# GpSimd rounds the weights' high parts beside the two top-256 searches of a hybrid attention block

## The chip, the cores and the metric

One core of a Trainium2 chip runs the kernel. Its engines are TensorE (PE; weight loads stand apart as PEld), VectorE (DVE), ScalarE (ACT), GpSimd (POOL) and SyncE (SP, which only issues DMAs). The metric is the device time of one execution in microseconds. The program is laid out by a scheduler: the Python code says what is to be done, and the scheduler sets the order in which each engine's instructions stand; on the chip each engine then works its queue in that order, and waits at its head.

## The reference, cut to what matters

The block takes x (1024 rows of 1024) through a mixer with two branches and through an MLP:

```python
h = rms_norm(x, g_mix[l]) * (1 + sc1) + sh1
proj = jnp.einsum('bsd,de->bse', h, w_in[l])
p_a, p_b = proj[..., :N_IN_A], proj[..., N_IN_A:]
...
# branch A, for each block of 128 queries: the 256 best keys by an index score
score_idx = jnp.where(key_pos[None, :] < limit[:, None], score_idx, -jnp.inf)
_, sel = lax.top_k(score_idx, topk)
...
# branch B: RWKV-7 time mixing on p_b, chunk by chunk
x = x + gt1 * jnp.einsum('bse,ed->bsd', mixed, w_out[l])
h = rms_norm(x, g_ffn[l]) * (1 + sc2) + sh2
u = jax.nn.relu(jnp.einsum('bsd,df->bsf', h, w_ff1[l]))
x = x + gt2 * jnp.einsum('bsf,fd->bsd', u * u, w_ff2[l])
```

## The kernel before, in words

The sequence is worked in two halves of 512 rows (`hf` 0 and 1). All matrices with a weight go through `dense` (line 406). It takes the weight in loads of 512 rows by 128 columns, and each load is split: `load_w` (line 393) fetches it with one DMA on SP into `wraw` (5 buffers), rounds it to a high part `whi`, and subtracts to get a low part `wlo` (4 buffers each). The activations are split in the same way (hh and hl, or uh and ul), and `dense` runs three matmuls of 128x128 by 512 columns for each 128 rows: hi with hi, hi with lo, lo with hi. So one load feeds 12 matmuls, and a group of two loads, 24 matmuls, fills one PSUM tile `ps_mm`, of which there are two. Before the change ACT makes every `whi` in one cast of 128x512 (line 399), and `wlo` is made on POOL in two subtractions of 128x256 (helper `InHalves`, line 136), in the second half's MLP on DVE (line 401). The table `LE` says which, by a number `GRP[0]` that the caller sets: 0 and 2 in `rwkv_proj` for the two halves (line 475), 1 and 3 in `attn_proj`, 4 and 5 in `out_proj`, 6 and 7 in `ffn`.

The top-256 choice is made in `indexer` (line 846) by a search over the 32 bits of the threshold: in each bit a candidate threshold is set, the scores at or above it are counted, and the bit is kept or dropped. Half of the query blocks are counted by DVE: `jk` (line 937 for the upper 16 bits on bf16 copies, line 939 for the lower 16 on the f32 scores and a zero tile), then `acc`, `pre` and `cand` on two columns (lines 952, 953, 928). The others are counted by ACT: `jka` (line 931), and then DVE makes `acca`, `prea` and `canda` (lines 946, 954, 929), and ACT's next count waits for `canda`. The first search, of `hf` 0, has one block on each engine. The second, of `hf` 1, has two on each (640 and 768 columns on DVE, 896 and 1024 on ACT). When the bits are done DVE builds the masks (lines 957 to 986), and `attention` starts.

The first search runs beside `rwkv_proj(1, hT1)`, that is 14 groups, 28 loads, of `w_in`; there ACT scales the group's result (`sh`, line 439) and DVE adds the shifted row (`shy`, line 443), which frees the PSUM tile. The second runs beside the first quarters of `ffn(0, ...)`. Its hidden columns go in four quarters `fg`; each has eight groups `f` of `w_ff1` (line 1114), whose result ACT takes out as relu (`ur`, line 1118), squares (line 1132) and rounds (`uh`, line 1133), and DVE subtracts (`ul`, line 1134), and then eight groups `d` of `w_ff2` (line 1139), whose result DVE adds to `xT` (line 1140). A quarter is 32 loads. A group `d` needs all eight uh and ul of its quarter.

Of the kernel before, what the change touches and what calls it, by code (L numbers as in the profile page):

```python
# [32 lines left out]
LS = 1  # L33
VB = (0, 1)
VB0 = 0
LE = 'gggggggv'
HE = 'aaaaaaaa'
DL = -1
PO = (1, 0, 2)
# [72 lines left out]
def body(tc, I, out, dbg=None):  # L112
    nc = tc.nc
    V, G, A, T = nc.vector, nc.gpsimd, nc.scalar, nc.tensor
# [26 lines left out]
    def mark(n):  # L141
        MK[0] = n
# [250 lines left out]
    def load_w(w, row0, col0, M):  # L393

        raw = wp.tile([128, 4, 128], F32, name="wraw", tag="wraw", bufs=WB[0])
        nc.sync.dma_start(raw[:, :, 0:M], w[row0:row0 + 512, col0:col0 + M].rearrange("(k p) n -> p k n", p=128))
        hi = wp.tile([128, 4, 128], F32R, name="whi", tag="whi", bufs=WB[1])
        lo = wp.tile([128, 4, 128], F32R, name="wlo", tag="wlo", bufs=WB[1])
        (A.copy if HE[GRP[0]] == "a" else V.tensor_copy)(hi[:, :, 0:M], raw[:, :, 0:M])  # L399
        GRP[1] ^= 1  # L400
        (V if LE[GRP[0]] == "v" or LE[GRP[0]] == "m" and GRP[1] else InHalves).tensor_tensor(lo[:, :, 0:M], raw[:, :, 0:M], hi[:, :, 0:M].bitcast(F32), ALU.subtract)  # L401
        return hi, lo

    GRP = [0, 0]
# [684 lines left out]
    def ffn(hf, xT, hT, fp, xp, hid, hooks={}):  # L1089
# [14 lines left out]
        def hook(unit):  # L1104
            for h in hooks.get(unit, ()):
                h()
                mark('ffn%d' % hf)
            GRP[0] = 6 + hf

        for fg in range(FF // 128 // GF):  # L1110
            uh, ul = [], []
            for f in range(GF):
                hook(16 * fg + f)
                ps = dense(I["w_ff1"], 0, 8, (fg * GF + f) * 128, 128,
                           lambda k: hT[0][:, k, :], lambda k: hT[1][:, k, :])
                r = fp.tile([128, HALF], F32, name="ur", tag="s2", bufs=sb(fp))
                if RL[hf] == "a":
                    A.activation(r, ps, AF.Relu)
                else:
                    V.tensor_scalar(r, ps, 0.0, None, ALU.max)  # L1120
                if f < 4:
                    ta, tb = (("shy", "fsq"), ("shy", "fsq"), ("sh1", "arn"), ("sh1", "cT"))[f]
                    a = dp.tile([128, HALF], F32R, name="uh", tag=ta, bufs=2)
                    b = dp.tile([128, HALF], F32R, name="ul", tag=tb, bufs=2 if f < 2 else 1)
                else:
                    a = hid.tile([128, HALF], F32R, name="uh", tag="uh", bufs=4)
                    b = hid.tile([128, HALF], F32R, name="ul", tag="ul", bufs=4)
                if SQ[hf] == "v":
                    A.activation(a, r, AF.Square)
                    V.tensor_tensor(r, r, r, ALU.mult)  # L1130
                else:
                    A.activation(r, r, AF.Square)
                    A.copy(a, r)  # L1133
                V.tensor_tensor(b, r, a.bitcast(F32), ALU.subtract)  # L1134
                uh.append(a)
                ul.append(b)
            for d in range(8):
                hook(16 * fg + 8 + d)
                ps = dense(I["w_ff2"], fg * GF * 128, GF, d * 128, 128, lambda k: uh[k], lambda k: ul[k])
                V.scalar_tensor_tensor(xT[:, d, :], ps, mod[:, 40 + d:41 + d], xT[:, d, :], ALU.mult, ALU.add)  # L1140
                if hf and fg == FF // 128 // GF - 1 and d in (5, 7):
                    store(d // 6)
# [217 lines left out]
```

## Time and profile before

| | |
|---|---|
| median of 3 runs | 1782.42 us (1778.94 to 1782.9) |
| the profiled execution: its own time | 1785.96 us |
| the profiled execution: its span, first to last instruction | 1784.2 us |
| granted TensorE clock, mean of the span | 0.972 |
| busy: PE, DVE, ACT, POOL | 1616.8, 1047.8, 878.1, 565.8 us |
| `whi` casts on ACT (line 399) | 384, 235.6 us |
| `wlo` subtractions on POOL (line 136) | 512, 404.4 us |
| first search: DVE's counts | about 414 to 469 us of the span |
| second search: DVE's counts, ACT's counts | about 890 to 995, to 1054 us |

Times below are microseconds from the start of the profiled execution's span. Busy time of PE is modelled and overlaps from one matmul to the next, so the number of matmuls in a stretch tells more than their busy time; a few records are missing. A wait is put down to the instruction that released it last. [...]

### The profile page before, as it was taken

The numbers are of one execution on the slowest core, as the hardware profiler recorded it, in microseconds if no ns is written. First come the engines' busy times: TensorE is split into PE (matmuls) and PEld (weight loads), VectorE is DVE, ScalarE is ACT, GpSimd is POOL, SyncE is SP. The second block draws the span as 40 slices with busy tenths as digits, with TensorE's granted clock in tenths as the row PEclk, the third lists the DMA queues.
The fourth block names the chain that finished last, engine by engine and source line by source line (L and its number), as shares of the span: only waits on it lengthen the run. The fifth ranks groups of instructions, "written<-read, shape, count | busy, mean of one in ns | idle before, by whom it ended". The sixth has DMA issues, their size and how long they took to land. (4 is left out here: it accounts for less than half of the span.)

```text
span 1784.2 us, 27312 instructions
## 1 busy us (share of the span) xinstructions
PE 1616.8 (91%) x9380; PEld 1217.4 (68%) x9380; DVE 1047.8 (59%) x2701; ACT 878.1 (49%) x1840; POOL 565.8 (32%) x751
## 2 busy tenths in 40 slices
PE   5997888988879988899968899999999999999998
PEld 2776655666655566666646676777886788888887
DVE  3786578559877676646999558763114233333333
ACT  3334364555637654535755865765235252525251
POOL 2555334353451344153224454113554300000000
PEclk9998999999999999999979999999999999999999
DMA  8895234333443441322112234324332333333332
GB/s 298 275 302 152 79 103 137 123 106 105 136 114 100 151 146 60 107 65 71 54 42 83 65 101 118 95 72 151 104 96 70 115 116 95 100 95 94 95 98 79
DMA packets 264018, 203.90 MB, mean 114 GB/s; under 512 B 17300, under 2 KB 218004, under 8 KB 263879
## 3 DMA queue, kind: packets, MB, share of 16 engines
q1 hardware_dynamic: 253122, 182.90, 34.1%
q10 hardware_dynamic: 10628, 19.24, 2.9%
q8 instruction: 74, 1.21, 0.3%
q14 instruction: 66, 0.53, 0.1%
q0 software_dynamic: 128, 0.01, 0.0%
HBM read 173.32 MB, written 28.78 MB: 113 GB/s over the span
## 5 line engine op out<-in xcount | busy, mean ns | idle before, releaser
L136 POOL TENSOR_TENSOR wlo<-wraw,whi 128x256 fp32r<-128x256 f32 x512 | 404.4, 813 | 590.7 <-ACT whi L399 493.2
L121 PE MATMUL ps_mm<-hh,whi 128*128 128x512 f32 (+1 forms) x1024 | 420.1, 411 | 27.2 <-ACT whi L399 7.1
L399 ACT CAST whi<-wraw 128x512 fp32r<-128x512 f32 x384 | 235.6, 616 | 423.9 <-PE ps_mm L121 385.9
L121 PE MATMUL ps_mm<-hl,whi 128*128 128x512 f32 (+1 forms) x1024 | 419.1, 409 | 4.2 <-DVE hl L345 1.9
L121 PE MATMUL ps_mm<-hh,wlo 128*128 128x512 f32 (+1 forms) x1024 | 414.2, 405 | 0.1
L121 PEld LDWEIGHTS ps_mm<-hh,whi 128*128 128x128 f32 (+1 forms) x1024 | 195.7, 192 | 75.0 <-ACT whi L399 16.7
L121 PEld LDWEIGHTS ps_mm<-hl,whi 128*128 128x128 f32 (+1 forms) x1024 | 196.7, 192 | 48.9 <-issue 6.8
L121 PEld LDWEIGHTS ps_mm<-hh,wlo 128*128 128x128 f32 (+1 forms) x1024 | 196.2, 192 | 42.8 <-issue 4.7
L121 PE MATMUL ps_mm<-uh,whi 128*128 128x512 f32 x512 | 204.9, 400 | 16.4 <-ACT whi L399 6.3
L121 PE MATMUL ps_mm<-ul,whi 128*128 128x512 f32 x512 | 204.4, 399 | 6.1 <-DVE ul L1134 6.1
L121 PE MATMUL ps_mm<-uh,wlo 128*128 128x512 f32 x512 | 203.9, 398 | 0.2
L401 DVE TENSOR_TENSOR wlo<-wraw,whi 128x512 fp32r<-128x512 f32 x128 | 88.2, 689 | 130.0 <-ACT whi L399 128.9
L931 ACT ACTIVATE jka<-sc,canda 128x1024 bf16<-128x1024 f32 (+1 forms) x93 | 90.2, 970 | 77.4 <-DVE canda L929 52.2
L121 PEld LDWEIGHTS ps_mm<-uh,whi 128*128 128x128 f32 x512 | 97.5, 191 | 43.1 <-issue 11.4
L121 PEld LDWEIGHTS ps_mm<-ul,whi 128*128 128x128 f32 x512 | 97.8, 191 | 28.9 <-DVE ul L1134 7.3
L121 PEld LDWEIGHTS ps_mm<-uh,wlo 128*128 128x128 f32 x512 | 97.6, 191 | 23.9 <-POOL wlo L136 1.7
L1140 DVE SCALAR_TENSOR_TENSOR xT<-ps_mm,mod,xT 128x512 f32<-128x512 f32 x64 | 47.8, 748 | 109.7 <-PE ps_mm L121 109.7
L1134 DVE TENSOR_TENSOR ul<-ur,uh 128x512 fp32r<-128x512 f32 x64 | 44.6, 697 | 80.1 <-ACT uh L1133 80.1
L1039 DVE CUSTOM_DVE_ANT_0 L<-ps_f,mk 128x512 f32<-128x512 f32 (+3 forms) x96 | 51.6, 551 | 26.6 <-PE ps_f L121 13.2
L1045 ACT ACTIVATE L<-L,m 128x128 f32<-128x128 f32 (+7 forms) x64 | 49.6, 776 | 19.5 <-DVE m L1042 14.4
L720 ACT COPY Ub<-ps_c 64x64 f32<-64x64 f32 x128 | 26.3, 205 | 65.5 <-DVE UV L718 56.9
L291 DVE SCALAR_TENSOR_TENSOR macc<-mraw,cs,macc 128x512 f32<-128x512 f32 x56 | 49.9, 890 | 10.0 <-DMA mraw<-in_w_ada_dram 8.5
(329 smaller groups left out, 2602.0 us busy)
## 6 DMA issues: line engine op xcount, KB each, us to landing
wraw<-in_w_ff_dram SPq DMA_DIRECT2D x256, 256.0 KB
wraw<-in_w_in_dram SPq DMA_DIRECT2D x92, 256.0 KB
mraw<-in_w_ada_dram SPq DMA_DIRECT2D x64, 256.0 KB
mraw<-in_w_ada_dram SPq DMA_DIRECT2D x16, 512.0 KB
wraw<-in_w_out_dram SPq DMA_DIRECT2D x32, 256.0 KB
rkvd<-shy ACTq DMA_DIRECT2D x24, 256.0 KB
xin<-in_x_dram SPq DMA_DIRECT2D x8, 512.0 KB
rt<-rnd SPq DMA_DIRECT2D x32, 128.0 KB
```

The source lines that it names most:

```text
L121: r = T.matmul(out, lhsT, rhs, start=start, stop=stop, **kw)
L136: G.tensor_tensor(o[:, c], a[:, c], b[:, c], op)
L291: V.scalar_tensor_tensor(acc, raw, c, acc, ALU.mult, ALU.add)
L399: (A.copy if HE[GRP[0]] == "a" else V.tensor_copy)(hi[:, :, 0:M], raw[:, :, 0:M])
L401: (V if LE[GRP[0]] == "v" or LE[GRP[0]] == "m" and GRP[1] else InHalves).tensor_tensor(lo[:, :, 0:M], raw[:, :, 0:M], hi[:, :, 0:M].bitcas ...
L720: (V.tensor_copy if CE[2] == "v" else A.copy)(Ub[h * 64:h * 64 + 64, h, :], pu[u, h * 64:h * 64 + 64])
L931: A.activation(jka[:, 0:width(b)], sc[b], AF.Sign, scale=-1.0, bias=0.0 if bit == 31 else canda.bitcast(F32)[:, i:i + 1], accum_out=ca[:, ...
L1039: V.tensor_tensor_reduce(L[:, c0:c0 + n], ps[:, 0:n], masks[b][:, c0:c0 + n], 1.0, -3e38, ALU.add, ALU.max, m2[:, pc:pc + 1])
L1045: A.activation(L[:, 0:W], L[:, 0:W], AF.Exp, bias=m2[:, 2:3], accum_out=m2[:, 3:4])
L1134: V.tensor_tensor(b, r, a.bitcast(F32), ALU.subtract)
L1140: V.scalar_tensor_tensor(xT[:, d, :], ps, mod[:, 40 + d:41 + d], xT[:, d, :], ALU.mult, ALU.add)
```

## The change

Where the first search runs (`GRP[0]` 2, all of `rwkv_proj(1, ...)`) and in the first two of the four quarters of `ffn(0, ...)` (a new group number 8), `whi` is no longer cast by ACT in one instruction of 512 columns but by POOL in two of 256. These are 28 and 64 loads. `wlo` stays on POOL in two subtractions. Nothing else in the code changes; the scheduler lays the program out anew.

```diff
-LE = 'gggggggv'
+LE = 'gggggggvg'
...
-        (A.copy if HE[GRP[0]] == "a" else V.tensor_copy)(hi[:, :, 0:M], raw[:, :, 0:M])
+        if GRP[0] in (2, 8):
+            for k in (0, 2):
+                G.tensor_copy(hi[:, k:k + 2, 0:M], raw[:, k:k + 2, 0:M])
+        else:
+            A.copy(hi[:, :, 0:M], raw[:, :, 0:M])
...
                 hook(16 * fg + f)
+                GRP[0] = 8 if not hf and fg < 2 else 6 + hf
                 ps = dense(I["w_ff1"], 0, 8, (fg * GF + f) * 128, 128,
...
                 hook(16 * fg + 8 + d)
+                GRP[0] = 8 if not hf and fg < 2 else 6 + hf
                 ps = dense(I["w_ff2"], fg * GF * 128, GF, d * 128, 128, lambda k: uh[k], lambda k: ul[k])
```

How the instructions stand in a row is shown at three places. The changed file is a few lines longer, so a line of it has a higher number (937 is 941, 939 is 943, 946 is 950, 952 is 956, 1118 is 1123, 1134 is 1139, 1140 is 1146).

POOL from the end of the second half's RWKV branch to the end of the second search, before (`ob` is the branch's output, `r` belongs to the norm ahead of the MLP, `klo` is a DMA that `attention(1)` needs):

```order
187 L136 TENSOR_TENSOR ob<-ob,bvs 128x256 x2
188 L136 TENSOR_TENSOR wlo<-wraw,whi 128x256 x12
189 L184 TENSOR_TENSOR r_8696<-r_8696,mhalf 128x4
190 L136 TENSOR_TENSOR wlo<-wraw,whi 128x256 x122
191 L995 DMA klo_9620<-in_spos_dram 1x16x64
192 L995 DMA klo_9621<-in_spos_dram 1x16x64
193 L136 TENSOR_TENSOR wlo<-wraw,whi 128x256 x128
```

POOL in the changed program, at the second search's end; above these rows the pairs of CAST and TENSOR_TENSOR alternate in the same way from row 241 on:

```order
361 L136 TENSOR_TENSOR wlo<-wraw,whi 128x256 x2
362 L401 CAST whi<-wraw 128x256 x2
363 L136 TENSOR_TENSOR wlo<-wraw,whi 128x256 x2
364 L401 CAST whi<-wraw 128x256
365 L999 DMA klo_9648<-in_spos_dram 1x16x64
366 L999 DMA klo_9649<-in_spos_dram 1x16x64
367 L401 CAST whi<-wraw 128x256
368 L136 TENSOR_TENSOR wlo<-wraw,whi 128x256 x2
```

Each load is now four instructions on POOL, two casts and two subtractions, one load after the other, and the DMA of `klo` stands between two casts, 63 instead of 67 loads behind the last `ob`.

ACT where DVE's counts of the second search end, before (`sc_8766` and `sc_8767` are the scores of ACT's two blocks; `ur` from `ps_mm` is the relu that frees a PSUM tile):

```order
956 L931 ACTIVATE jka,ca<-sc_8766,canda 128x896
957 L399 CAST whi<-wraw 128x512
958 L931 ACTIVATE jka,ca<-sc_8767,canda 128x1024
959 L399 CAST whi<-wraw 128x512
960 L931 ACTIVATE jka,ca<-sc_8766,canda 128x896
961 L1118 ACTIVATE ur<-ps_mm 128x512
962 L931 ACTIVATE jka,ca<-sc_8767,canda 128x1024
963 L1132 ACTIVATE ur<-ur 128x512
964 L399 CAST whi<-wraw 128x512
965 L931 ACTIVATE jka,ca<-sc_8766,canda 128x896
966 L1133 CAST uh<-ur 128x512
```

ACT at the same place in the changed program:

```order
897 L935 ACTIVATE jka,ca<-sc_8794,canda 128x896
898 L935 ACTIVATE jka,ca<-sc_8795,canda 128x1024
899 L935 ACTIVATE jka,ca<-sc_8794,canda 128x896
900 L1123 ACTIVATE ur<-ps_mm 128x512
901 L935 ACTIVATE jka,ca<-sc_8795,canda 128x1024
902 L1137 ACTIVATE ur<-ur 128x512
903 L935 ACTIVATE jka,ca<-sc_8794,canda 128x896
904 L1138 CAST uh<-ur 128x512
905 L935 ACTIVATE jka,ca<-sc_8795,canda 128x1024
906 L1123 ACTIVATE ur<-ps_mm 128x512
```

The casts of `whi` are gone from between the counts. A group of the MLP now stands beside three counts; in the rows before it stands beside two or three, with two casts more.

DVE where the first quarter passes from `w_ff1` to `w_ff2`, before (`ul` is that of the quarter's last group `f`, `xT` that of its first group `d`; `top_9198` and `top_9200` are the bf16 copies of DVE's two blocks):

```order
1576 L952 TENSOR_SCALAR acc<-cv 128x2
1577 L954 TENSOR_TENSOR prea<-prea,acca 128x2
1578 L953 TENSOR_TENSOR pre<-pre,acc 128x2
1579 L929 SCALAR_TENSOR_TENSOR canda<-prea,xma 128x2
1580 L1134 TENSOR_TENSOR ul<-ur,uh 128x512
1581 L928 SCALAR_TENSOR_TENSOR cand<-pre,xmh 128x2
1582 L937 TENSOR_SCALAR jk,cv<-top_9198,cand 128x640
1583 L937 TENSOR_SCALAR jk,cv<-top_9200,cand 128x768
1584 L1140 SCALAR_TENSOR_TENSOR xT<-ps_mm,mod,xT 128x512
```

DVE at the same place in the changed program:

```order
1579 L941 TENSOR_SCALAR jk,cv<-top_9226,cand 128x640
1580 L1139 TENSOR_TENSOR ul<-ur,uh 128x512
1581 L941 TENSOR_SCALAR jk,cv<-top_9228,cand 128x768
1582 L950 TENSOR_SCALAR acca<-ca 128x1
1583 L956 TENSOR_SCALAR acc<-cv 128x2
1584 L957 TENSOR_TENSOR pre<-pre,acc 128x2
1585 L932 SCALAR_TENSOR_TENSOR cand<-pre,xmh 128x2
1586 L941 TENSOR_SCALAR jk,cv<-top_9226,cand 128x640
1587 L1146 SCALAR_TENSOR_TENSOR xT<-ps_mm,mod,xT 128x512
```

Counted by the `acc` rows, `ul` has moved ahead by one bit of the search, and `xT` stands in the same bit; the seven `xT` that follow stand two bits apart in both programs. Where DVE's own counts end, 21 instead of 23 and 50 instead of 52 `canda` rows stand above in the program before and the changed one, in that order, for the first search and the second.

## Rows read from the trace of the kernel before

**Rows 1.** Windows view: busy us (instructions) by engine, PEclk, DMA share, GB/s.

```profile
405.00:475.00 70.00, 59.97 (x234) 45.44 (x232) 64.69 (x283) 40.50 (x89) 26.94 (x35) 0.93 0.39 113
...
885.00:940.00 55.00, 39.87 (x140) 30.03 (x139) 53.05 (x160) 28.75 (x54) 17.86 (x22) 0.81 0.16 48
940.00:988.00 48.00, 41.86 (x171) 32.58 (x170) 46.81 (x129) 27.32 (x50) 21.02 (x25) 0.96 0.24 72
988.00:1041.00 53.00, 46.26 (x189) 35.60 (x188) 20.92 (x79) 49.02 (x92) 22.45 (x31) 0.97 0.25 73
...
1055.00:1091.00 36.00, 28.91 (x123) 22.33 (x122) 35.52 (x55) 8.20 (x13) 21.30 (x23) 1.00 0.44 125
...
1250.00:1784.00 534.00, 525.08 (x2312) 423.69 (x2310) 175.85 (x257) 197.43 (x328) 81.81 (x111) 1.00 0.33 96
```

**Rows 2.** Waits of PE, 880 to 1000, then 1000 to 1060: total, times, longest.

```profile
PE ps_mm L121 <- ACT whi L399: 9.7, 3, 3.9
PE ps_mm L121 <- DVE ul L1134: 4.4, 1, 4.4
...
PE ps_mm L121 <- ACT whi L399: 3.7, 2, 2.1
```

**Rows 3.** Timeline of PE after the first of these waits: start, us, instruction [idle before].

```profile
905.52 0.80 PE L121 MATMUL ps_mm<-hh,whi 128*128 128x512 f32 x1 [3.34 <-ACT whi L399]
...
906.54 0.63 PE L121 MATMUL ps_mm<-hh,wlo 128*128 128x512 f32 x1
...
906.97 0.63 PE L121 MATMUL ps_mm<-hh,whi 128*128 128x512 f32 x1
```

**Rows 4.** Timeline of ACT ahead of it.

```profile
901.66 1.04 ACT L931 ACTIVATE jka<-sc,canda 128x896 bf16<-128x896 f32 x1 [3.61 <-DVE canda L929]
...
904.86 0.61 ACT L399 CAST whi<-wraw 128x512 fp32r<-128x512 f32 x1
```

**Rows 5.** Line 1134 on DVE, 885 to 935: ns min/median/max, first and last start.

```profile
L1134 DVE TENSOR_TENSOR ul<-ur,uh x4: 684/686/1130, 899.0 to 930.5; 128x512 fp32r<-128x512 f32 x4
```

**Rows 6.** Timeline of DVE: `acc` beside POOL's work, then `acc` and a count without.

```profile
946.23 0.58 DVE L952 TENSOR_SCALAR acc<-cv 128x2 int32<-128x2 f32 x1
...
951.17 0.15 DVE L952 TENSOR_SCALAR acc<-cv 128x2 int32<-128x2 f32 x1
...
951.75 0.88 DVE L939 SCALAR_TENSOR_TENSOR jk<-sc,cand,zer 128x640 bf16<-128x640 f32 x1
```

**Rows 7.** Groups of DVE, 885 to 988: xcount | busy us, mean ns | idle before.

```profile
L939 DVE SCALAR_TENSOR_TENSOR jk<-sc,cand,zer 128x640 bf16<-128x640 f32 x14 | 14.6, 1043 | 0.4
...
L952 DVE TENSOR_SCALAR acc<-cv 128x2 int32<-128x2 f32 x29 | 9.3, 320 | 0.4
L953 DVE TENSOR_TENSOR pre<-pre,acc 128x2 int32<-128x2 int32 x28 | 8.0, 286 | 0.6
...
L928 DVE SCALAR_TENSOR_TENSOR cand<-pre,xm 128x2 int32<-128x2 int32 x14 | 3.7, 266 | 0.3
```

**Rows 8.** POOL's line 136, 885 to 988, then 405 to 471: ns min/median/max.

```profile
L136 POOL TENSOR_TENSOR wlo<-wraw,whi x47: 722/737/1492, 885.1 to 986.8; 128x256 fp32r<-128x256 f32 x47
...
L136 POOL TENSOR_TENSOR wlo<-wraw,whi x30: 717/737/1185, 410.6 to 468.7; 128x256 fp32r<-128x256 f32 x30
```

**Rows 9.** POOL's line 681, a copy of 256 columns: ns min/median/max.

```profile
L681 POOL COPY TT<-D x16: 387/393/400, 174.6 to 732.8; 32x256 f32<-32x256 f32 x16
```

**Rows 10.** Timeline of ACT late in the second search: two counts of the same block.

```profile
1022.10 1.03 ACT L931 ACTIVATE jka<-sc,canda 128x896 bf16<-128x896 f32 x1
...
1025.80 1.04 ACT L931 ACTIVATE jka<-sc,canda 128x896 bf16<-128x896 f32 x1
```

**Rows 11.** Timeline of DVE late in the first search, when its counts are done.

```profile
472.63 0.15 DVE L946 TENSOR_SCALAR acca<-ca 128x1 int32<-128x1 f32 x1 [0.94 <-ACT jka L931]
...
474.29 0.15 DVE L946 TENSOR_SCALAR acca<-ca 128x1 int32<-128x1 f32 x1 [0.94 <-ACT jka L931]
```

**Rows 12.** Waits of PE, 1060 to 1250.

```profile
PE ps_mm L121 <- DVE xT L1140: 7.1, 4, 2.7
```

## The prediction

> **What bounds the kernel now.** I read the windows view first. From 1250 us to the end PE is never idle for long: 2312 recorded matmuls in 534 us, one each 0.231 us at clock 1.00 [rows 1]. There the kernel is bound by PE, and nothing that the change touches lies there. So the change is worth what it alters in the stretches where PE falls short of that rate, and these are beside the searches. From 885 to 988, where DVE and ACT count the second search, PE ran 140 and 171 matmuls; at 0.231 us that is 72 us of work in 103 us, so 31 us are lost. From 988 to 1041, when DVE has done its counts and ACT still has some, 189 matmuls are 44 us of work in 53, and 9 us are lost [rows 1].
>
> Then who is full there. DVE is busy 53.05 of 55 and 46.81 of 48 us from 885 to 988, ACT only 28.75 and 27.32; from 988 to 1041 ACT is busy 49.02 of 53 and DVE 20.92; while the masks are built, 1055 to 1091, DVE is busy 35.52 of 36. The first search has the same picture: DVE 64.69 of 70 us, ACT 40.50, POOL 26.94 [rows 1].
>
> Then what PE waited for. In the second search three waits of 9.7 us together end with ACT's `whi`, and later 3.7 us more; but 4.4 us end with DVE's `ul` [rows 2]. The first wait shows the mechanism that the change goes at: the cast of `whi` stands in ACT's queue behind a count that had waited 3.61 us for `canda` [rows 4], so PE idled 3.34 us, and after that its matmuls started 0.43 us apart, the lower of its two clock levels [rows 3].
>
> **The change part by part.** ACT gives up 92 casts, 28 beside the first search and 64 beside the second and its masks; POOL gets 184 of half the size. No DMA and no byte is added. SP's queue still issues `wraw` as soon as `wlo` has freed a buffer. The DMA of `klo` on POOL stands four loads earlier in PE's work, and casts now stand behind it as well as subtractions; as the search also ends earlier in PE's work, I cost it at nothing.
>
> What a cast takes on POOL the trace does not show. The nearest row is a copy of as many columns on fewer partitions, 0.39 us [rows 9]; the other end is the subtraction, with two inputs, at 0.74 us [rows 8]. I take 0.39, as a cast reads one input like the copy. A load is then 2 x 0.39 + 2 x 0.74 = 2.26 us on POOL, while PE needs 12 x 0.231 = 2.77 us for it. POOL can follow, and with four buffers it can run ahead.
>
> Second search, 885 to 988. The PE waits on `whi` go: 9.7 us. I count no gain for that, because something else is late next. The last `ul` of the quarter runs at 930.5 us [rows 5], every group `d` needs it, and DVE has no idle time before it. In the order of the change `ul` comes one bit of the search earlier, and the first `xT` comes in the same bit as before, the next seven two bits apart as before. PE has two PSUM tiles, so from there on it moves as DVE's bits move. What counts is whether DVE gets through its bits faster, and it gets slower, for two reasons.
>
> The first is POOL. Beside POOL's work an `acc` of two columns took 0.58 us, and 0.15 without it; a count of 640 columns takes 0.88 undisturbed [rows 6]. The means of the stretch say how much of this there is: `acc` 29 x (0.320 - 0.15) = 4.9 us, `pre` 28 x (0.286 - 0.15) = 3.8, `cand` 14 x (0.266 - 0.15) = 1.6, the 640-column count 14 x (1.043 - 0.88) = 2.3, together 12.6 us [rows 7]. In the stretch POOL made 47 halves of `wlo` [rows 8], so each cost DVE 0.27 us. A cast holds POOL for about half as long. I take 0.12 us for each, between nothing (the copy of rows 9 ran undisturbed every time, though on few partitions) and 0.27 (as for a subtraction): 47 x 0.12 = 5.6 us, from 0 to 12.7. The second reason: ACT, with fewer casts, is two bits further when DVE is done (52 `canda` rows above instead of 50), and each bit is four small DVE instructions of 0.15 us: 1.2 us. Together **+6.8 us**.
>
> [...]
>
> First search. POOL made 30 halves of `wlo` from 405 to 471 [rows 8], so 30 casts come in: 30 x 0.12 = 3.6 us (0 to 8.1), and 1.2 us for two more bits of ACT's search within DVE's. In return ACT has two bits fewer left when DVE is done, and there a bit takes 1.66 us, from one `acca` to the next [rows 11]: -3.3 us. What follows (the second half's RWKV head and the first attention) waits for both. Together **+1.5 us**.
>
> The tail of the second search, 988 to 1041. ACT's counts of one block stand 3.70 us apart there, with two other instructions of ACT between the two counts [rows 10]. In the order of the change a group of the MLP stands beside three counts, 1.5 x 3.70 = 5.5 us, and PE needs 24 x 0.231 = 5.5 us for a group. So ACT and PE fit each other, without the 3.7 us of waits on `whi` and what the clock loses behind them; but the small DVE instructions between ACT's counts now meet a POOL that is busy four fifths of the time. Of the 9 us lost I take 4 back, from 0 to 9: **-4 us**.
>
> The masks, 1055 to 1091. About 9 loads, 18 casts: 18 x 0.12 = 2.2 us on a DVE that is full, and PE waits there for `xT` already, 7.1 us [rows 12]. Not all of it reaches PE: **+1.5 us** (0 to 4.9).
>
> The sum is 6.8 + 1.5 - 4 + 1.5 = +5.8 us. The profiled execution, at 1785.96 us, would come to 1791.8. It lies 3.5 us above the median of the runs, so against 1782.42 the forecast is **1788 us**. A measurement of this kernel can tell about 0.2%, 3.6 us, from no change.
>
> **The rivals.** *Faster: PE's waits on ACT were the loss.* If the last `uh` and `ul` of the quarter were late only since PE was late, the 9.7 and 3.7 us of waits on `whi` go and stay gone, 13.4 us, and the time is 1769; if DVE takes back a third of them, 1774. For it: the queue of rows 4, and a clock of 0.81 from 885 to 940 [rows 1] that short waits would lift. Against it: DVE's 99.9 busy us of 103. It decides at `ul`: is DVE idle ahead of it or not.
>
> *No change.* If a cast costs DVE some 0.05 us, half of what I take or less, the three terms of casts fall from 11 to about 5 us and the sum to zero: 1782. For it: rows 9. [...]
>
> *Slower by far: POOL becomes the bound.* A cast that takes 0.74 us or more, as a subtraction does, makes a load 2.96 us on POOL against PE's 2.77, before any waiting for DVE, and some of POOL's halves took up to 1.49 us [rows 8]. Then each cast costs DVE 0.27 us, 95 x 0.15 = 14 us more, and PE waits on POOL in the tail and the masks, some 25 loads by 0.2 us, 5 us: 1807. It decides from 0.65 us a cast, where 2 x 0.65 + 2 x 0.74 passes 2.77.
>
> That the change does not do what it says is out: in its order POOL has the 184 casts and ACT 292 instead of 384.
>
> **How the numbers follow.** The forecast gets 0.43, the faster rival 0.27, no change 0.22, the bound on POOL 0.08. The forecast's own range, from its bounds with some of them at the middle, is 1783 to 1797; I put 0.03 of it within 0.2%. So faster by over 0.2% has 0.27, within 0.2% 0.25, slower 0.48. The range from 1773 to 1803 takes in most of the faster rival and leaves out its far end and the bound on POOL.
>
> **What the profile of the changed kernel would show.** Right: no PE wait on a `whi` of ACT beside the searches; the wait for `ul` ahead of the first group `d` longer than 4.4 us; `acc`, `pre` and `cand` with higher means than rows 7; casts of about 0.39 us on POOL; DVE's counts of the second search done later, against their start, than the 105 us from 890 to 995; fewer lost us while ACT counts alone. Wrong: DVE idle ahead of `ul` (then PE was the bound, and the faster rival holds); means as in rows 7 (a cast costs DVE nothing); PE waits on `whi` or `wlo` of POOL (the bound on POOL). A loss in the stretch between the two searches, 500 to 885, where only the order changes, would be outside all of these.

## The result and the profile after

The changed kernel takes 1800.94 us (median of four runs, 1799.79 to 1803.83), beside 1782.66 us for the kernel before: a ratio of 1.0096, 95% interval 1.007 to 1.0121. The forecast was 1788 us, slower. It is slower, by 18.3 us where the sum had 5.8. One run of the kernels below, 2199.37 us with memsets, was in a slow state (granted clock 0.652) and is left out of that kernel's ratio and of its median.

The profiled execution after took 1800.26 us, its span is 1798.4, its granted clock 0.968. It lies near its median, while the profiled execution before lay 3.3 us above its own, so the two traces show 14.3 us of the 18.3.

Where they part is read best from instructions that both kernels have. One line's instructions, kernel before: count, ns min/median/max, first and last start. `acc` comes once in each bit of DVE's search, `shy` and `ul` take up the result of a group that PE has finished.

```profile
L952 DVE TENSOR_SCALAR acc<-cv x31: 135/153/156, 416.6 to 469.8; 128x1 int32<-128x1 f32 x31
...
L443 DVE SCALAR_TENSOR_TENSOR shy<-ps_mm,prm,sh x14: 736/749/751, 383.5 to 486.4; 128x511 f32<-128x511 f32 x14
...
L952 DVE TENSOR_SCALAR acc<-cv x31: 155/169/704, 893.9 to 995.6; 128x2 int32<-128x2 f32 x31
...
L1134 DVE TENSOR_TENSOR ul<-ur,uh x8: 683/692/693, 996.6 to 1039.2; 128x512 fp32r<-128x512 f32 x8
...
L1134 DVE TENSOR_TENSOR ul<-ur,uh x8: 677/692/693, 1326.3 to 1380.9; 128x512 fp32r<-128x512 f32 x8
```

The same view of the changed kernel, with the first quarter's `ul`, which answers to [rows 5], and the new casts:

```profile
L956 DVE TENSOR_SCALAR acc<-cv x31: 134/153/155, 417.2 to 472.2; 128x1 int32<-128x1 f32 x31
...
L447 DVE SCALAR_TENSOR_TENSOR shy<-ps_mm,prm,sh x14: 732/746/752, 384.7 to 490.8; 128x511 f32<-128x511 f32 x14
...
L1139 DVE TENSOR_TENSOR ul<-ur,uh x4: 685/686/809, 905.6 to 937.6; 128x512 fp32r<-128x512 f32 x4
...
L956 DVE TENSOR_SCALAR acc<-cv x31: 152/236/708, 899.7 to 1005.8; 128x2 int32<-128x2 f32 x31
...
L1139 DVE TENSOR_TENSOR ul<-ur,uh x8: 678/692/1230, 1006.9 to 1051.2; 128x512 fp32r<-128x512 f32 x8
...
L1139 DVE TENSOR_TENSOR ul<-ur,uh x8: 676/692/693, 1340.5 to 1395.1; 128x512 fp32r<-128x512 f32 x8
...
L401 POOL CAST whi<-wraw x53: 388/403/1155, 894.7 to 1005.8; 128x256 fp32r<-128x256 f32 x53
```

By these rows the work of PE is behind by 1.2 us at the first `shy` beside the search, by 4.4 at the last, by 6.6 at the first `ul` that the second search holds up (899.0, 905.6), by 10.3 when DVE's counts are over (996.6, 1006.9), by 12.0 at the end of the tail (1039.2, 1051.2), and by 14.2 behind the masks (1326.3, 1340.5); from there on nothing is added. DVE's 31 bits of the second search take 106.1 us from first to last `acc` where they took 101.7, those of the first 55.0 where they took 53.2.

The granted clock and the busy times, windows view of the changed kernel (columns as in [rows 1]), beside DVE's counts, in the tail as far as ACT counts, and beside the masks:

```profile
888.00:1008.00 120.00, 92.59 (x352) 71.41 (x351) 116.98 (x328) 57.74 (x100) 76.99 (x112) 0.89 0.20 60
...
1005.00:1054.00 49.00, 41.52 (x172) 32.41 (x171) 21.75 (x66) 40.66 (x73) 34.25 (x59) 0.96 0.27 81
...
1066.00:1102.00 36.00, 30.50 (x122) 23.07 (x121) 32.96 (x44) 6.46 (x11) 25.48 (x34) 0.91 0.50 132
```

In the traces of both kernels the granted clock stands at 0.50 or at 1.00, so a value between them means that a stretch had some of each. In the kernel before it is 0.50 from 905.5 to 908 us, where the matmuls of [rows 3] start 0.43 us apart, and 1.00 from 908.5 to 910, where they start 0.23 us apart.

DVE is full beside its counts, 116.98 of 120 us, as it was before. ACT is busy for only 57.74 of them, and even in the tail, where it had been busy 49.02 of 53 us [rows 1], for 40.66 of 49. POOL is busy for 77 of the 120 us and is no bound.

What PE waits for, from 888 to 1008 and then from 1008 to 1066 (total, times, longest):

```profile
PE ps_mm L121 <- ACT ur L1123: 6.9, 2, 4.5
PE ps_mm L121 <- DVE ul L1139: 6.3, 2, 4.4
...
PE ps_mm L121 <- ACT uh L1138: 4.9, 1, 4.9
...
PE ps_mm L121 <- ACT uh L1138: 3.8, 1, 3.8
PE ps_mm L121 <- ACT ur L1123: 3.3, 3, 1.7
PE ps_mm L121 <- POOL whi L401: 0.4, 1, 0.4
```

The 13.4 us of waits on `whi` [rows 2] are gone, all of them. In their place stand 18.9 us of waits on ACT's `ur` and `uh`, where there were 3.8 before. These stand in the same queue behind the same counts, and a group of the MLP needs them as it needed `whi`. What ACT did with the time that it got back is in its own waits, before (882 to 1054):

```profile
ACT jka L931 <- DVE canda L929: 36.0, 17, 4.4
ACT jka L931 <- DVE cand L928: 6.1, 2, 4.5
ACT jka L931 <- DVE acc L952: 3.8, 1, 3.8
ACT jka L931 <- DVE pre L953: 2.6, 1, 2.6
```

and after (888 to 1054):

```profile
ACT jka L935 <- DVE canda L933: 65.5, 29, 5.5
```

ACT's counts waited 48.5 us for DVE's small instructions, and now wait 65.5. Over the whole of the second search the relief of ACT went into waiting for DVE; the tail by itself comes further down.

What the casts do to DVE shows on single instructions. The timeline of the changed kernel, DVE:

```profile
950.98 0.31 DVE L957 TENSOR_TENSOR pre<-pre,acc 128x2 int32<-128x2 int32 x1
951.21 0.15 DVE L933 SCALAR_TENSOR_TENSOR canda<-prea,xma 128x2 int32<-128x2 int32 x1
951.33 0.32 DVE L932 SCALAR_TENSOR_TENSOR cand<-pre,xm 128x2 int32<-128x2 int32 x1
```

and POOL beside it:

```profile
950.87 0.76 POOL L401 CAST whi<-wraw 128x256 fp32r<-128x256 f32 x2
```

Both `pre` and `cand` begin 0.1 us into one of the two casts, take 0.31 and 0.32 us instead of 0.15, and end about 0.01 us after that cast does. So it is with all 15 `acc`, `pre` and `cand` of the second search that began beside a cast and took over 0.29 us: they end 7 to 23 ns after it. Added up between the first and the last `acc`, the time above 0.155 us of the six kinds of small instructions (`acc`, `pre`, `cand`, `acca`, `prea`, `canda`) that began beside a cast is 3.4 us; beside subtractions it is 12.1 us, and in the kernel before 13.3. The groups of DVE from 895 to 1006, which answer to [rows 7]:

```profile
L957 DVE TENSOR_TENSOR pre<-pre,acc 128x2 int32<-128x2 int32 x30 | 8.8, 295 | 0.5
L956 DVE TENSOR_SCALAR acc<-cv 128x2 int32<-128x2 f32 x31 | 8.7, 279 | 0.3
L932 DVE SCALAR_TENSOR_TENSOR cand<-pre,xm 128x2 int32<-128x2 int32 x16 | 6.2, 389 | 0.2
```

`cand` has risen from 266 to 389 ns, `pre` from 286 to 295; `acc` has fallen from 320 to 279. POOL's instructions meet some of DVE's more often than before and others less.

### The profile page after: what moved, and what is told of

It is laid out like the page before. It is cut to its first block, busy times and chain, and to the rows that moved or that the text cites. A ratio compares the mean times of both kernels' runs of the same rounds, so it can differ in the third digit from the quotient of the medians.

```text
span 1798.4 us, 27395 instructions
## 1 busy us (share of the span) xinstructions
PE 1621.6 (90%) x9380; PEld 1221.5 (68%) x9380; DVE 1062.3 (59%) x2701; ACT 834.7 (46%) x1748; POOL 654.5 (36%) x935
## 5 line engine op out<-in xcount | busy, mean ns | idle before, releaser
L403 ACT CAST whi<-wraw 128x512 fp32r<-128x512 f32 x292 | 179.8, 618 | 384.2 <-PE ps_mm L121 353.0
L401 POOL CAST whi<-wraw 128x256 fp32r<-128x256 f32 x184 | 94.0, 538 | 149.4 <-PE ps_mm L121 148.7
L121 PEld LDWEIGHTS ps_mm<-uh,whi 128*128 128x128 f32 x512 | 98.7, 193 | 48.5 <-ACT uh L1138 9.5
L1043 DVE CUSTOM_DVE_ANT_0 L<-ps_f,mk 128x512 f32<-128x512 f32 (+3 forms) x96 | 51.9, 553 | 27.3 <-PE ps_f L121 13.3
```

Source lines behind the costliest of these rows:

```text
L121: r = T.matmul(out, lhsT, rhs, start=start, stop=stop, **kw)
L401: G.tensor_copy(hi[:, k:k + 2, 0:M], raw[:, k:k + 2, 0:M])
L403: A.copy(hi[:, :, 0:M], raw[:, :, 0:M])
L1043: V.tensor_tensor_reduce(L[:, c0:c0 + n], ps[:, 0:n], masks[b][:, c0:c0 + n], 1.0, -3e38, ALU.add, ALU.max, m2[:, pc:pc + 1])
```

## The experiments

Theory: the casts on POOL are paid by DVE, which is the bound beside the searches, so they lengthen the search and PE with it, while the relief of ACT is worth little. Rival 1: the new order is the loss, as the scheduler, which takes ACT to be free, sets more counts ahead of each group. Rival 2: POOL is late itself. Rival 3: PE's waits on `whi` were worth their 13 us and the casts cost twice that.

All ratios are against the kernel before, run on the same chip between the runs of the kernel in question. Its own median there was 1784.0 to 1784.7 us, with runs from 1777.8 to 1796.6. Diffs are against the changed kernel where nothing else is said.

**The casts without the relief.**

```diff
         if GRP[0] in (2, 8):
             for k in (0, 2):
-                G.tensor_copy(hi[:, k:k + 2, 0:M], raw[:, k:k + 2, 0:M])
-        else:
-            A.copy(hi[:, :, 0:M], raw[:, :, 0:M])
+                G.tensor_copy(lo[:, k:k + 2, 0:M], raw[:, k:k + 2, 0:M])
+        A.copy(hi[:, :, 0:M], raw[:, :, 0:M])
```

> ACT keeps all its casts of whi, and POOL makes the 184 casts besides, into wlo, which its subtraction then overwrites; the order of every engine is that of the kernel before but for these casts. Theory (the casts are paid by DVE, some 0.1 us each, and DVE is the bound beside the searches): about 95 casts lie there, +8 to +14 us, so 1791 to 1797, with DVE's counts of the second search taking 109 to 112 us where they took 105. Rival 1 (the new order is the loss: the scheduler puts the MLP's groups behind more of the search's counts, which do not come sooner): 1782 to 1785, as the order is the old one. Rival 2 (POOL itself is late): PE waits on wlo of POOL, 5 us or more beside the searches.

Measured: 1807.19 us, ratio 1.0117 [1.0092, 1.0142]. Rival 1 says nothing can happen here, since the order is the old one, and this is the largest loss but one of all. DVE's second search is longer by as much as in the changed kernel, 106.0 us with 51 casts beside it:

```profile
L955 DVE TENSOR_SCALAR acc<-cv x31: 153/244/702, 902.9 to 1008.9; 128x2 int32<-128x2 f32 x31
...
L401 POOL CAST wlo<-wraw x51: 390/403/1131, 897.5 to 1007.9; 128x256 fp32r<-128x256 f32 x51
```

So 4.4 us for 51 to 53 casts, 0.08 to 0.09 us each; the small instructions that began beside a cast were held for 4.3 us here, those beside subtractions for 13.0, as before. That the loss passes the change's own is not at odds with this: here PE still has its waits on `whi` too (9.4 us from 891 to 1011). Rival 2 asked for 5 us or more of waits of PE on POOL's `wlo`, and from 885 to 1110 there are 1.6. The search was forecast to take 109 to 112 us counted from its start; from first to last `acc` it gained 4.4. The rest of the 21 us lies elsewhere: PE is 2.1 us late at the first `shy`, 6.5 at the last, 14.8 at the end of the tail and 22.1 behind the masks; how the casts cause this part is not shown.

**The relief without the casts.** `hic` is one tile of 128x128 that is made once; `wlo` is the weight less this constant, so POOL works as before.

```diff
         if GRP[0] in (2, 8):
-            for k in (0, 2):
-                G.tensor_copy(hi[:, k:k + 2, 0:M], raw[:, k:k + 2, 0:M])
+            hi = hic.unsqueeze(1).to_broadcast([128, 4, 128])
```

> Nobody makes whi in the two groups: a constant tile of 128x128 stands in its place, so the output is not the reference's; POOL still makes wlo. ACT is relieved of the 92 casts and POOL gets none. Theory (the casts on POOL are the loss, the relief is worth little as DVE is the bound): 1776 to 1783. Rival 1 (the order is the loss; this kernel has the order of the changed one beside the second search): 1790 to 1800, slower than before although it does less. Rival 3 (PE's waits on whi were worth their 13 us, and the casts on POOL cost twice that): 1767 to 1772.

Measured: 1789.23 us, ratio 1.0029 [1.0012, 1.0045]. ACT's 92 casts are taken away and put nowhere, and the kernel does not become faster; it is a little slower, less than rival 1 asked for and more than the theory did. Rival 3 is out. The trace says why nothing is gained:

```profile
L957 DVE TENSOR_SCALAR acc<-cv x31: 153/169/589, 895.0 to 995.7; 128x2 int32<-128x2 f32 x31
...
L1140 DVE TENSOR_TENSOR ul<-ur,uh x8: 685/713/1064, 996.2 to 1038.8; 128x512 fp32r<-128x512 f32 x8
...
ACT jka L936 <- DVE canda L934: 57.7, 29, 5.2
...
PE ps_mm L121 <- DVE ul L1140: 6.1, 2, 4.4
PE ps_mm L121 <- ACT ur L1124: 5.5, 2, 3.9
PE ps_mm L121 <- ACT uh L1139: 4.9, 1, 4.9
```

DVE's bits take 100.7 us, one less than before. ACT waits for `canda` instead of working (882 to 1042), and PE waits for `ur` and `uh` instead of `whi` (883 to 999), just as in the changed kernel. So these waits come with the relief and its order, not with POOL. In the tail the eight `ul` take 42.6 us from first to last, as they did in the kernel before, and 44.3 in the changed kernel: there too the relief brings nothing, and 1.7 us come with the casts. The profiled run is the quickest of its twelve (1784.88), and PE stands in it where it stood before; where the 0.3% of the median lies is not seen in it.

**One search at a time.**

```diff
-        if GRP[0] in (2, 8):
+        if GRP[0] == 2:
```

> POOL makes whi beside the first search only (28 loads). In the profile of the changed kernel PE comes out of the first search 4.4 us later than before, and 4.1 us later it still stands at 820 us. Theory: that part stays, 1785 to 1788. Rival (it is made up for later, where the second search starts from wherever PE stands): 1781 to 1784.

Measured: 1791.61 us, ratio 1.0035 [1.0018, 1.0052]. The part of the first search stays to the end, 6.2 us by the ratio; it is not made up for.

```diff
-        if GRP[0] in (2, 8):
+        if GRP[0] == 8:
```

> POOL makes whi in the first two quarters of the MLP only (64 loads), beside the second search and the masks. From 890 us to the end of the masks the changed kernel lost about 9 us more than before in the profiles, and 18 us in all by the medians. Theory: the two parts add up, 1790 to 1796. Rival (the loss beside the second search comes from the shifted start after the first): 1782 to 1786.

Measured: 1797.53 us, ratio 1.0062 [1.0042, 1.0083], some 11 us. The two add up to 0.97%, and the change has 0.96%. The rows of `acc` in the second search are the cleanest of the whole study, without casts there (first row, first search only) and with them:

```profile
L956 DVE TENSOR_SCALAR acc<-cv x31: 153/169/706, 899.3 to 1001.0; 128x2 int32<-128x2 f32 x31
```

```profile
L956 DVE TENSOR_SCALAR acc<-cv x31: 151/237/710, 890.6 to 997.2; 128x2 int32<-128x2 f32 x31
```

101.7 against 106.6 us. The first search of the second kernel takes the 53.2 us of the kernel before.

**The order of the tail put back.** ACT's counts of a list wait in the order for the relu of their group; nothing waits on the chip that did not.

```diff
+PINS = (66, 69, 72, 74, 78, 80, 84, 87)
...
-                A.activation(jka[:, 0:width(b)], sc[b], AF.Sign, scale=-1.0,
+                counts.append(A.activation(jka[:, 0:width(b)], sc[b], AF.Sign, scale=-1.0,
...
-                    A.activation(r, ps, AF.Relu)
+                    rel = A.activation(r, ps, AF.Relu)
+                    if not hf and fg == 1:
+                        tc.add_manual_dep(counts[PINS[f]].ins, rel.ins.name,
+                                          mybir.DependencyInfo(mybir.DependencyClass.NoSync, mybir.DependencyReason.DATA), reason="order")
```

> The changed kernel, but in the tail of the second search each group's relu on ACT is held at the place among ACT's counts where it stood before the change (66, 69, 72, 74, 78, 80, 84, 87 counts ahead of it instead of 70 to 92). Theory (what the casts cost DVE is the loss): as the changed kernel, 0.8 to 1.1% over before. Rival 1 (groups that stand behind more counts are the loss): 0.5% over before or less.

Measured: 1800.23 us, ratio 1.0085 [1.0067, 1.0102]. That is the changed kernel's loss within the intervals, and above what rival 1 allowed.

```profile
L1144 DVE TENSOR_TENSOR ul<-ur,uh x8: 678/686/841, 1016.1 to 1055.0; 128x512 fp32r<-128x512 f32 x8
```

The trace of this kernel gives rival 1 a small part: from the last `ul` ahead of the second search (894.4) to the last of the tail it takes 160.6 us, where the changed kernel takes 163.6 and the kernel before 157.2. So about 3 of 6.4 us come back there, in single executions; in the ratios it is 0.11%, less than the intervals can tell. The places among the counts of the tail are not the bulk of what the change lost by.

**The tail alone**, where ACT still counts and DVE does not.

```diff
-        if GRP[0] in (2, 8):
+        if GRP[0] == 8:
...
-                GRP[0] = 8 if not hf and fg < 2 else 6 + hf
+                GRP[0] = 8 if not hf and fg == 1 else 6 + hf
...
-                GRP[0] = 8 if not hf and fg < 2 else 6 + hf
+                GRP[0] = 6 + hf
```

> POOL makes whi only for the groups f of the second quarter, 16 loads, about where ACT still counts and DVE is idle half of the time. Theory: the casts cost little there and ACT is the full engine, so 0 to 0.2% under before. Rival 1 (the scheduler answers with more counts ahead of each group, 89 instead of 87 ahead of the last): 0.1 to 0.3% over before.

Measured: 1794.31 us, ratio 1.0049 [1.0031, 1.0067]. The theory's number is wrong, and rival 1's is too small. The first reason is that the casts do not lie where their groups do:

```profile
L401 POOL CAST whi<-wraw x16: 390/400/1127, 970.0 to 993.5; 128x256 fp32r<-128x256 f32 x16
```

POOL runs ahead of the groups, so half of the 32 casts come before DVE's last bit (this row ends at 996), and its bits take 104.2 us, 2.5 longer. The second is in the waits of ACT, 995 to 1051:

```profile
ACT jka L935 <- DVE canda L933: 7.0, 9, 1.7
```

In the kernel before ACT waited 4.4 us for `canda` from 995 to 1053, and here 7.0, although DVE has time there. That POOL holds the small instructions between two counts fits this, and in the tail of the changed kernel `canda` rose from 231 to 345 ns. PE's waits on ACT go from 5.7 us (`whi` 3.7, `ur` 2.0) to 7.3 (`ur` 4.6, `uh` 2.7). How large a share of the 0.49% all this is can't be read off, since the profiled run is again the quickest (1786.64).

**The first quarter alone.**

```diff
-        if GRP[0] in (2, 8):
+        if GRP[0] == 8:
...
-                GRP[0] = 8 if not hf and fg < 2 else 6 + hf
+                GRP[0] = 8 if not hf and fg < 1 else 6 + hf
```

(The last edit stands in both places.)

> POOL makes whi in the first quarter of the MLP only, 32 loads, nearly all beside DVE's counts of the second search. Theory: DVE's counts from their second bit to their last take 105 to 107 us, as in every kernel with casts on POOL there, where they took 101 to 102 without, and the time is 0.2 to 0.45% over before. Rival (the loss lies in the tail and the masks alone): within 0.1% of before.

Measured: 1792.34 us, ratio 1.0046 [1.0029, 1.0063], and DVE's bits take 103.9 us (896.6 to 1000.5) with 34 casts beside them: 2.2 us longer than without, less than the 105 to 107 expected, which counted all casts of that stretch as the first quarter's. The rest are the tail's, from 970 on. In DVE's time the two parts add up (2.2 and 2.5 against the 4.9 us of both quarters), in the kernel's time they do not: 0.46 and 0.49% by themselves, and 0.62% together with the masks' part. The excess of 0.33% is about as large as the intervals; whether there is one is not shown. Nor is the price of a cast the same everywhere: 2.2 us for 34 casts is 0.06 us each, 2.5 us for 16 in the kernel with the tail alone is 0.16.

**One cast of 512 columns.**

```diff
-            for k in (0, 2):
-                G.tensor_copy(hi[:, k:k + 2, 0:M], raw[:, k:k + 2, 0:M])
+            G.tensor_copy(hi[:, :, 0:M], raw[:, :, 0:M])
```

> The change with one cast of 512 columns on POOL in place of two of 256. If DVE pays for the time that POOL is at work, the casts together take as long, and the time is that of the change, 0.8 to 1.1% over before. If DVE pays once for each instruction of POOL that it meets, the half of the casts' part is gone, 0.3 to 0.7% over before. If it pays more for a long one (it is held to its end), 1.1 to 1.6%.

Measured: 1807.59 us, ratio 1.0128 [1.0098, 1.0157]. DVE does not pay per instruction met, or half would be gone; its bits of the second search take 106.3 us beside 24 such casts, where they took 106.1 beside 53 of the short ones.

```profile
L955 DVE TENSOR_SCALAR acc<-cv x31: 152/170/708, 900.2 to 1006.5; 128x2 int32<-128x2 f32 x31
...
L400 POOL CAST whi<-wraw x92: 606/614/2114, 339.6 to 1091.5; 128x512 fp32r<-128x512 f32 x92
```

One premise of the expectation falls: a cast of 512 columns takes 0.614 us and not twice 0.402, so POOL is at work for less time in all (71.8 us against 94.0) and the kernel is no faster for it. A longer hold seems to cost DVE more for its length; the intervals of this kernel and of the change overlap, so it is not shown.

**A write in place of the cast.** As the first experiment; the diff is against that one:

```diff
-                G.tensor_copy(lo[:, k:k + 2, 0:M], raw[:, k:k + 2, 0:M])
+                G.memset(lo[:, k:k + 2, 0:M].bitcast(F32), 0.0)
```

> As the kernel with casts besides those of ACT (ratio 1.0117), but each cast of POOL is a memset of the same 256 columns, which reads nothing; the subtraction overwrites it. If what DVE pays is for POOL being at work in its memory at all, the loss goes with the length of the memsets, which are a little shorter than the casts: 0.6 to 1.1% over before. If it is reading that meets DVE, 0 to 0.3%.

Measured: 1793.38 us, the median of eleven runs, ratio 1.0057 [1.0034, 1.008], about half of what the casts cost in the same place.

```profile
L401 POOL MEMSET wlo<- x184: 301/312/591, 342.7 to 1078.6; 128x256 f32 x184
...
L955 DVE TENSOR_SCALAR acc<-cv x31: 153/300/1170, 892.5 to 997.0; 128x2 int32<-128x2 f32 x31
```

The loss is just under the 0.6 to 1.1% of the one expectation and above the 0 to 0.3% of the other. The memsets are shorter, 0.312 against 0.403 us, 0.77 of it, and the loss is 0.49 of the casts' loss; DVE's bits take 104.5 us. But the memsets themselves hold next to nothing. All six `cand` (two tensors read) that began beside a memset took 0.16 us and ended before it did; in the first experiment all eight that began beside a cast took 0.30 to 0.32 us and ended 8 to 17 ns after it. The small instructions that began beside a memset were held for 0.6 us together, and those beside a subtraction for 19.2, where the kernel before has 13.3. So what DVE's small instructions pay here they pay to the subtractions, which stand at other moments than before and hold them longer; that this is the whole of the 0.57% is not shown.

**Other places among the counts.** The changed kernel with `if GRP[0] == 99`, which never holds, so that all casts are on ACT as before; `UH`, `UL_` and `XT` number the count of ACT (`counts`) or the `cand` of DVE (`cands`), over both searches, ahead of which a group's `uh`, `ul` and `xT` must stand.

```diff
+UH = (0, 0, 0, 0, 35, 36, 38, 39, 58, 61, 64, 67, 70, 73, 76, 79)
+UL_ = (0, 0, 0, 0, 33, 35, 37, 39, 55, 57, 58, 60, 0, 0, 0, 0)
+XT = (41, 43, 45, 47, 48, 50, 52, 53)
...
+    def before(at, inst, later):
+        if at:
+            tc.add_manual_dep(later[at].ins, inst.ins.name,
+                              mybir.DependencyInfo(mybir.DependencyClass.NoSync, mybir.DependencyReason.DATA), reason="order")
...
+                if not hf and fg < 2:
+                    before(UH[8 * fg + f], cast, counts)
+                    before(UL_[8 * fg + f], sub, cands)
...
+                if not hf and not fg:
+                    before(XT[d], add, cands)
```

> The kernel before, all casts of whi on ACT, but the groups of the MLP are held at earlier places among the counts of the second search: the first quarter's groups f every two bits of DVE's search instead of every four, its groups d every 1.7 instead of 2, and the second quarter's groups f from there on. If the places among the counts set PE's pace (2.6 us a bit, so 10.5 us a group where PE needs 5.5), some 20 us of the 31 us that PE loses from 885 to 988 come back: 0.6 to 1.1% under before. If DVE's or ACT's work is the bound as a sum, what is gained there is given back in the tail and the masks: within 0.2% of before. If PE's waits stall the search, slower.

Measured: 1780.28 us, ratio 0.9972 [0.9958, 0.9985]: faster than both kernels.

```profile
L1148 DVE TENSOR_TENSOR ul<-ur,uh x4: 678/682/685, 898.9 to 919.2; 128x512 fp32r<-128x512 f32 x4
...
L965 DVE TENSOR_SCALAR acc<-cv x31: 157/169/726, 896.0 to 1014.7; 128x2 int32<-128x2 f32 x31
...
L1148 DVE TENSOR_TENSOR ul<-ur,uh x8: 678/692/810, 984.2 to 1031.2; 128x512 fp32r<-128x512 f32 x8
```

The groups f that took 10.5 us each (899.0 to 930.5 for three [rows 5]) take 6.8, without a cast moved: their pace was set by their places among the counts. PE is 12.4 us ahead when the second quarter begins (984.2 against 996.6). But DVE has more of the groups' `ul` and `xT` beside its bits, which take 118.7 us instead of 101.7, and most of the lead is given back in the tail (8.0 us are left at 1031.2 against 1039.2) and behind it. Of the 20 us looked for, 5 are kept.

The same places with POOL's casts in the two quarters, against the kernel just above:

```diff
-        if GRP[0] == 99:
+        if GRP[0] == 8:
```

> The same places, with whi of the first two quarters made on POOL in two casts a load. Theory (each cast costs DVE some 0.1 us): 0.4 to 0.7% over the kernel with these places and the casts on ACT. Rival 3 (with the groups closer together ACT's casts are what PE waits for, and POOL takes that away): 0.2% or more under that kernel.

Measured: 1782.83 us, ratio 0.9994 [0.9978, 1.0011], 0.22% over the kernel with these places and casts on ACT. The sign is the theory's and the size half of it, about as large as the intervals. Whether the relief of ACT buys something with the groups this dense, or the casts cost less there, these runs do not tell apart; DVE's bits take 120.9 us, 2.2 more, beside 68 casts: 0.03 us each.

Milder places, for the first quarter alone, all casts on ACT, against the first kernel of this kind:

```diff
-UH = (0, 0, 0, 0, 35, 36, 38, 39, 58, 61, 64, 67, 70, 73, 76, 79)
-UL_ = (0, 0, 0, 0, 33, 35, 37, 39, 55, 57, 58, 60, 0, 0, 0, 0)
-XT = (41, 43, 45, 47, 48, 50, 52, 53)
+UH = (0, 0, 0, 0, 35, 37, 38, 40, 0, 0, 0, 0, 0, 0, 0, 0)
+UL_ = (0, 0, 0, 0, 33, 35, 37, 40, 0, 0, 0, 0, 0, 0, 0, 0)
+XT = (42, 44, 46, 48, 50, 52, 54, 56)
```

> The kernel before, casts on ACT, with milder pins than the first of that kind: the first quarter's groups f stand two to three bits of DVE's search apart instead of four, its groups d two bits apart as before, three to four bits earlier, and nothing is pinned behind them. Theory (the places set PE's pace, but DVE's sum gives most of it back): 0.2 to 0.5% under before. Rival (only the dense places of the whole tail bring the gain): within 0.15% of before.

Measured: 1783.26 us, ratio 0.9988 [0.9969, 1.0006]: within the rival's 0.15%, and no difference that can be told from none. The gain of the first of these kernels needs the dense places behind the first quarter too.

## Why the prediction was right in its direction and too small

**The bound, and what is late next: right.** Beside the counts DVE is full before and after. The waits on `whi` went, and `ul` and others were late in their place. Two of the signs named for this came out only in part: the two waits for `ul` make 6.3 us, but the longest is 4.4 us as before, and the mean of `acc` fell. The first rival, that they would stay gone and save 13.4 us, is refuted by the kernel that has the relief alone.

**The price of a cast: right in kind, a little too high.** The step took 0.12 us for each of 47 casts, 5.6 us, with 0 and 12.7 as its ends, and 1.2 for two more of ACT's bits. DVE's bits became 4.4 us longer with 53 casts, 0.083 each. PE lost 4.7 us between the last `ul` ahead of the search (882.0 before, 887.6 after) and the first behind it. The term was +6.8. The price moves with what the casts meet, from 0.03 to 0.16 us in the kernels above.

The cast's own time was taken from a copy as 0.39 us, and its median is 0.402. What a cast costs DVE depends on what it meets: in the second search the 26 small instructions that were held beside a cast end 7 to 25 ns after it. All 14 `pre` and `cand` (two tensors read) that began beside a cast of the second search were held (0.23 to 0.32 us, where they take 0.16 alone), none of the 11 `acca` (one tensor, one column; 0.154 us at most), and the counts on the bf16 copies (one tensor) took 0.88 us for 640 columns whether POOL worked beside them or not. `acc`, with one tensor of two columns, was held 9 times of 10; in the first search, where it has one column, it never took over 0.155 us.

The shortest cast of 256 columns took 0.388 us, and the shortest of 512 took 0.606. So 256 columns more cost 0.218 us, and by these two lengths I estimate that some 0.17 us of a cast do not go with its columns.

**The tail: wrong, and the largest part of the miss that the traces show.** The step was "Of the 9 us lost I take 4 back": ACT without its casts was to fit PE, group by group. The trace has +1.7 us there (10.3 to 12.0), 5.7 us off. The relief of ACT is worth nothing even when it is free (ratio 1.0029, and 42.6 us for the tail's `ul` with it and without), although ACT had been busy 49.02 us of 53 there. Its counts go in a chain: a count on ACT, three small instructions on DVE, the next count. With less to do it waited more for `canda`, in the tail 8.8 us of 49 where it had been 4.4 of 58 (before, 995 to 1053; after, 1005 to 1054):

```profile
ACT jka L931 <- DVE canda L929: 4.4, 5, 1.3
...
ACT jka L935 <- DVE canda L933: 8.8, 11, 2.0
```

That this chain sets the pace in the tail is the reading that fits; no kernel here shortened it alone. In the forecast I had named what could spoil the term, "the small DVE instructions between ACT's counts now meet a POOL that is busy four fifths of the time", and let it weigh only in taking 4 of 9.

**The first search: too small, by the same mistake.** The step was 3.6 + 1.2 - 3.3 = +1.5 us, where -3.3 was again ACT's relief. DVE's counts took 1.8 us longer (55.0 against 53.2), less than the 4.8 counted, but ACT's did not end sooner (71.2 us from DVE's first `acc` to the last `acca`, 71.0 before), and PE came out 3.2 us later than it went in (1.2 to 4.4). Alone this part costs 0.35%, 6.2 us.

**The masks: right in size, and in part by luck.** +1.5 was forecast, and 2.2 us are added from 1039 us to the end (12.0 to 14.2). But the way was to be PE's waits for `xT`, and these fell from 7.1 us [rows 12] to 5.0. Instead PE waited 3.8 us for `uh` at 1051, and the granted clock was 0.91 from 1066 to 1102 where it had been 1.00 [rows 1]. DVE did pay there, its four scans for the masks took 1.5 us more together (7.6 to 9.0); how much of it reached PE is not shown.

**Between the searches**, where I expected nothing, 1.2 us more (4.4 at the last `shy`, 5.6 at the last `ul` ahead of the second search), and 1.2 before the first `shy`. Kernels with the same order there differ by as much.

So the traces have 14.3 us against 5.8 forecast, and two gains that did not come, 4 and 3.3 us, are most of the gap. The rest of the 18.3 is that the profiled execution before was 3.3 us above its median; the forecast took that off, rightly, but two single executions can't carry a statement on the last 4 us.

**The rivals.** That POOL becomes the bound is out, though not by much: its casts take 0.40 us and PE's matmuls waited 0.4 us for one, once. PE's weight loads have 12.8 us of waits put down to `whi` (8 times), but in six of the seven from 960 us on the `xT` or `ur` that freed the PSUM tile ended 0.05 to 0.5 us after the cast. No change is out too.

**Open.** Where the 0.3% of the relief alone lies, where most of the loss of the casts alone lies, and whether the first quarter's part and the tail's together exceed that of both quarters. The two halves of the change do not add up either: casts alone 1.17%, relief alone 0.29%, both 0.96%. Casts for the groups d beside the masks were not tried alone.

## What to carry to other kernels

An engine that is busy nine tenths of a stretch need not be its bound if it works in turns with another: here taking work from it lengthened its waits (for `canda`, from 4.4 us of 58 to 8.8 of 49), so before such a gain is counted, follow the loop from one of its instructions to the next and see whose instructions lie in it. Work that goes to an idle GpSimd can be paid by VectorE: here all 14 `pre` and `cand`, which read two tensors, and 9 of 10 `acc` of two columns were held until 7 to 25 ns after the end of the cast they began beside, and DVE's bits grew by 0.08 us on average for a cast of 0.40. Where in-order queues interleave two streams, the place of one among the other can set its pace, and moving that place can be worth more than moving the work: here earlier places took a group from 10.5 to 6.8 us and the kernel to a ratio of 0.9972, and moving the casts gave 1.0096.

## What the runs showed that I had not expected

- The holds beside the casts of the changed kernel's second search end 7 to 25 ns after the cast, and a cast of 512 columns (0.614 us) takes POOL less than two of 256 (0.804) and is not better for DVE (bits of 106.3 us and 106.1).
- The holding goes both ways: in the changed kernel's second search 16 of the 19 casts that began beside a count on the f32 scores and the zero tile took 0.64 to 1.16 us and ended 0.26 us after that count; of 10 that began beside a count on the bf16 copies none took over 0.45.
- Memsets, which read nothing, cost half as much as casts in the same place (0.57% against 1.17%), though they held the small instructions for 0.6 us only; POOL's subtractions beside them held more than before (19.2 against 13.3 us).
- The first search's bits take 53.2 us from first to last `acc` to a tenth in all seven kernels that leave that place as it was, while whole runs of one kernel differ by up to 19 us (1777.8 to 1796.6).
